# Down projection: running sums copied into accumulator banks by ScalarE, in place of sums on VectorE and by transfers

## Chip, core and metric

The kernel runs on one core of a Trainium2 chip. The metric is device time in microseconds (us) of one execution; lower is better. TensorE (PE) does the matrix products, VectorE (DVE) and ScalarE (ACT) work on tiles, GpSimd (POOL) and SyncE (SP) issue transfers here. Every engine runs its own instructions strictly in the order in which they stand in the program, and an instruction waits until what it reads is written and what it overwrites has been read.

## What is computed

One layer of a diffusion step, for two groups of 128 tokens each (prompt and sample) and a model width of 2048. Cut to what matters:

```python
h  = rms_norm(x, norm1_w) * (1 + sc1) + sh1
qa, ka, va, qb, kb, vb, ga, gb = project_heads(h, w_in, ...)
oa, ob = ...                     # windowed attention, neighbourhood attention
x  = x + g1 * (sigmoid(ga) * (oa @ w_br_a) + sigmoid(gb) * (ob @ w_br_b)) @ w_out
h2 = rms_norm(x, norm2_w) * (1 + sc2) + sh2
x  = x + g2 * (square(relu(h2 @ w_up)) @ w_down)      # w_up 2048x8192, w_down 8192x2048
```

The change lies in the last line. Every fp32 product is made of three matmuls over rounded parts: high x high, high x low, low x high. A weight tile `raw` of 128x1024 is therefore split: ScalarE copies it to `wH` (rounded, L93), VectorE subtracts to get `wL` (L241).

## The kernel before

**Steps.** The whole layer is one list of 456 weight steps, `wsteps`. A step is one 512 KB weight tile: SyncE loads it, ScalarE and VectorE split it, TensorE does 12 matmuls of 128x512 with it. `run()` writes the instructions out step by step. Three tables set the order: `RUN[i]` (how many steps ahead the loads stand), `LOOK[i]` (how many steps ahead the two splitting instructions stand) and `LO_DMA` (steps whose low part is made by a negated copy on ScalarE, L247, and an accumulating transfer issued by GpSimd). `at(i, fn)` places other work behind the matmuls of step i; `load_at(i, fn)` places loads ahead of it. Further tables (`T_PAIR`, `P_PAIR`, `DOTS`, `JOBS` and so on) say at which step smaller pieces of work stand.

**The MLP.** The up projection makes 16 column blocks of 512 (`up0` to `up15`), the down projection consumes them in 8 pieces of two blocks. After block 0 and 1 the program runs in turn: pair p+1 of the up projection (16 steps, some of them in a form with seven products where eight are usual, at the positions in `FAST`), then piece p of the down projection. In the seven-product form, VectorE first makes sums of weight tiles (`t`, `raw`, L1172 to L1182), and TensorE collects in banks `Q1` to `Q7`; at a pair's end the banks are put together into `up` (ScalarE `up<-Q`, then VectorE L1217 and ScalarE's Relu and Square, L1223). The result is turned to stationary form through ScalarE copies (`pla`, `fTa`, `aNH`) and transposing transfers, with VectorE's low parts (`aNL`, L97).

**The down projection.** A piece has four column units n of 512 columns. A unit is 4 steps, 48 matmuls, into two accumulator banks (`acc`, one for each token group). Four banks of the pool `pacc` are handed round among the units and the pairs' first Q banks. The sum over the 8 pieces is kept in SBUF tiles `dsum[n]`. When unit (p, n) is done, `evac` takes its two banks:

- piece 0: ScalarE copies both to `dsum[n]` (L93);
- pieces 1 to 6, the 10 units in `SUM_DMA` (unit number 4p+n): ScalarE copies both to a further tile, and a transfer issued by GpSimd adds that tile to `dsum[n]` (L1261);
- the other 14 units: VectorE adds each bank to `dsum[n]` (L1257);
- behind piece 6, `gate_sum(n)`: VectorE multiplies `dsum[n]` by the gate (L1238) and adds it to the residual `x1[n]` (L1239);
- piece 7: `resid` multiplies the bank by the gate and adds it to `x1[n]` (L904, L905), and the result is stored. The last unit is `last_unit`, which ends with one bank ahead of the other.

The gate tiles (`gate_bc`) and `x1` (`x1_back`) are loaded six steps before the end of each unit of piece 6.

Of the kernel before, what the change touches and what calls it, by code (L numbers as in the profile page):

```python
# [51 lines left out]
XS_AT = {1: 13, 2: 18, 3: 29}  # L52
POST = {('kvA', 0): [67, 70, 75], ('qA', 0): [70, 73, 78], ('qA', 1): [72, 74, 80], ('kB', 0): [77, 83, 90], ('qB', 0): [82, 84, 93], ('kB', 1): [86, 91, 93], ('qB', 1): [90, 93, 97]}
JOBS = [[79, 80, 80, 87, 93], [81, 83, 88, 90, 93], [87, 87, 89, 90, 99], [93, 93, 96, 99, 102], [96, 97, 100, 105, 112], [102, 103, 107, 112, 123], [105, 107, 111, 118, 123], [112, 115, 118, 121, 123]]
SS_AT = [43, 51, 73, 75, 139, 139]
T_AT = [4, 4]
PREP_IN = [6, 7]
DOTS = [33, 39, 42, 43, 47, 47, 48, 49, 52, 54, 55, 57, 60, 62, 69, 70, 73, 77, 80, 84, 90, 91, 92, 92, 94, 98, 101, 103, 103, 105, 108, 110, 111, 112, 115, 118, 120, 121, 122, 122, 126, 127, 128, 129, 130, 132, 132, 136, 137, 138, 138, 143, 144, 147, 147, 150, 153, 155, 157, 161, 164, 167, 170, 172, 173, 174, 175, 176, 177, 178, 179, 182]
DOTS2 = [230, 232, 234, 235, 236, 237, 240, 243, 255, 263, 265, 269, 270, 288, 301, 301, 307, 328, 328, 331, 333, 334, 358, 360, 361, 363, 366, 368, 391, 391, 395, 399]
STAT_AT = [-1, 0, 10, 16]  # L60
T_PAIR = [[8, 9], [6, 8], [8, 9], [7, 8], [10, 11], [8, 9], [12, 11]]
P_PAIR = [[4, 2], [2, 4], [3, 4], [1, 3], [6, 6], [3, 3], [6, 5]]
M_TE = (3,)
# [8 lines left out]
def tile_hybrid_step(ctx: ExitStack, tc: tile.TileContext, a):  # L72
# [210 lines left out]
    def mm3(acc, stat, st, first, last, order=(0, 1)):  # L283

        wh, wl = st["hl"]
        for k in range(2):
            kk = 2 * st["half"] + k
            for tb in order:
                sh, sl = stat(kk, tb)
                f, l = first and k == 0, last and k == 1  # L290
                pe.matmul(acc[tb], sh, wh[:, k, :], start=f, stop=False)  # L291
                pe.matmul(acc[tb], sh, wl[:, k, :], start=False, stop=False)  # L292
                pe.matmul(acc[tb], sl, wh[:, k, :], start=False, stop=l)  # L293
# [219 lines left out]
    def unit(w, c0, ktiles, stat, evac, key, order="both"):  # L513
# [377 lines left out]
    x1 = {}  # L891
# [159 lines left out]
    def last_unit(w, c0, ktiles, stat, evac_s, key):  # L1051
# [4 lines left out]
        def mms(q, tb):  # L1056
            wh, wl = box["hl"][q]
            for k in range(2):
                sh, sl = stat(q // 2)(2 * (q % 2) + k, tb)
                pe.matmul(box["acc"][tb], sh, wh[:, k, :], start=q == 0 and k == 0, stop=False)  # L1060
                pe.matmul(box["acc"][tb], sh, wl[:, k, :], start=False, stop=False)
                pe.matmul(box["acc"][tb], sl, wh[:, k, :], start=False, stop=q == n - 1 and k == 1)

        for j, k0 in enumerate(ktiles):
            def mm(st, j=j):
                q = 2 * j + st["half"]
                if q == 0:
                    box["acc"] = [bank("acc", pacc) for _ in range(2)]
# [38 lines left out]
    def up_pair(p):  # L1107
# [32 lines left out]
        for pos, is_fast in enumerate(kinds):  # L1140
# [50 lines left out]
            def mm_y(st, b=b, j=j, pos=pos, end=end):  # L1191
# [42 lines left out]
    def gate_sum(n):  # L1234

        d = dsum.pop(n)
        for s in range(2):
            dve.tensor_tensor(d[:, s, :], d[:, s, :], gbc["g2", n][:, s, :], op=OP.mult)  # L1238
# [259 lines left out]
```

## Time and profile before

| what | value |
| --- | --- |
| median of 3 runs | 1333.61 us (1331.23, 1333.61, 1334.71) |
| span of the profiled execution | 1331.3 us |
| TensorE busy | 1316.0 us, 99% |
| TensorE weight loads busy (beside matmuls) | 1067.0 us, 80% |
| VectorE busy | 1190.2 us, 89% |
| ScalarE busy | 800.8 us, 60% |
| GpSimd busy | 54.6 us, 4% |
| traffic | 392 MB, mean 295 GB/s |

The span of the profiled execution is its own time from the first to the last instruction, and for this execution it is the only time recorded; it lies 2.3 us under the median of the runs. Matmuls overlap in the records (each shows 0.39 us, the next starts 0.227 us later), so a busy TensorE has to be read by the distance from one start to the next.

### The profile page before, as it was taken

What the parts mean: (1) busy time and instruction counts of PE and PEld (TensorE: products, weight loads), DVE (VectorE), ACT (ScalarE), POOL (GpSimd) and SP (SyncE); (2) the same over time, 40 slices, a digit from 0 to 9 for tenths busy, and PEclk for the clock granted to TensorE, in tenths of its full rate; (3) what the DMA queues carried; (4) which work ended last, traced back from release to release, by engine and by line L of the source; (5) the groups of instructions that cost most, each with busy time, mean ns of one, the idle gap of its engine ahead of it and who ended that gap; (6) DMA issues with size and microseconds to landing.
All of it is one profiled execution on the core that took longest, in us unless ns stands there. A gap on an engine that the chain in (4) does not pass through costs nothing.

```text
span 1331.3 us, 18039 instructions
## 1 busy us (share of the span) xinstructions
PE 1316.0 (99%) x6411; PEld 1067.0 (80%) x6412; DVE 1190.2 (89%) x1546; ACT 800.8 (60%) x979; POOL 54.6 (4%) x64
## 2 busy tenths in 40 slices
PE   8999999999999999999999999999999999999998
PEld 4777778788888878888888888888888888877887
DVE  4699999988898999999779998998999999989685
ACT  5534443476656446635677866758577576676660
POOL 0000000521000000000000000000000000000000
PEclk9999999999999999999999999999999999999999
DMA  9999998986589999996578876988798696878962
GB/s 374 409 409 408 409 401 300 384 277 240 177 329 355 381 392 356 354 367 214 191 230 280 281 254 215 291 273 266 235 296 255 237 301 206 311 195 291 331 213 98
DMA packets 148267, 392.24 MB, mean 295 GB/s; under 512 B 51793, under 2 KB 53009, under 8 KB 148177
## 3 DMA queue, kind: packets, MB, share of 16 engines
q1 hardware_dynamic: 144448, 378.16, 78.8%
q0 software_dynamic: 3584, 12.85, 5.0%
q8 instruction: 50, 0.82, 0.3%
q14 instruction: 41, 0.33, 0.1%
q10 hardware_dynamic: 144, 0.08, 0.0%
HBM read 367.16 MB, written 8.68 MB: 282 GB/s over the span
## 4 chain that ended last, share of the span: by engine, by line
PE 92%; DMA 4%; DVE 2%; ACT 1%; issue 1%; SPq 0%; DVEq 0%; ACTq 0%
PE acc L291 16%; PE acc L292 16%; PE acc L293 16%; PE Q L1117 6%; PE Q L1119 6%; PE Q L1118 6%; PE acc L391 4%; PE acc L392 4%; PE acc L393 4%; DMA araw<-in_w_pair 3%; PE ps_ada L308 2%; PE ps_S L707 1%; PE Z L1119 1%; PE Z L1117 1%; PE Z L1118 1%; DMA aT<-in_w_adaT 1%
## 5 line engine op out<-in xcount | busy, mean ns | idle before, releaser
L241 DVE TENSOR_TENSOR wL<-raw,wH 128x1024 fp32r<-128x1024 f32 x375 | 446.6, 1225 | 72.0 <-ACT wH L93 67.9
L93 ACT ACTIVATE wH<-raw 128x1024 fp32r<-128x1024 f32 (+1 forms) x393 | 392.8, 1044 | 128.3 <-PE acc L392 23.3
L391 PE MATMUL acc<-wH,hH 128*128 128x512 f32 x276 | 109.1, 395 | 0.0
L393 PE MATMUL acc<-wH,hL 128*128 128x512 f32 x276 | 107.5, 390 | 0.0
L392 PE MATMUL acc<-wL,hH 128*128 128x512 f32 x276 | 107.5, 389 | 0.0
L291 PE MATMUL acc<-wH,hH 128*128 128x512 f32 x256 | 101.4, 396 | 0.0
L293 PE MATMUL acc<-wH,hL 128*128 128x512 f32 x256 | 99.7, 390 | 0.0
L292 PE MATMUL acc<-wL,hH 128*128 128x512 f32 x256 | 99.7, 390 | 0.0
L1327 DVE CUSTOM_DVE_ANT_0 aT<-aT,cB,cols 128x1024 f32<-128x1024 f32 x56 | 71.7, 1286 | 0.2
L1327 DVE CUSTOM_DVE_ANT_0 junk<-aT,cB,cols 128x1024 bf16<-128x1024 f32 x56 | 71.4, 1280 | 0.0
L93 ACT ACTIVATE tH<-t 128x1024 fp32r<-128x1024 f32 x33 | 35.0, 1061 | 58.0 <-DVE t L1172 55.4
L391 PEld LDWEIGHTS acc<-wH,hH 128*128 128x128 f32 x276 | 51.8, 188 | 13.6 <-issue 2.5
L393 PEld LDWEIGHTS acc<-wH,hL 128*128 128x128 f32 x276 | 51.8, 188 | 11.0
L392 PEld LDWEIGHTS acc<-wL,hH 128*128 128x128 f32 x276 | 51.8, 188 | 10.4
L293 PEld LDWEIGHTS acc<-wH,hL 128*128 128x128 f32 x256 | 48.0, 188 | 10.2
L291 PEld LDWEIGHTS acc<-wH,hH 128*128 128x128 f32 x256 | 48.1, 188 | 9.8 <-ACT sq L622 0.4
L292 PEld LDWEIGHTS acc<-wL,hH 128*128 128x128 f32 x256 | 48.1, 188 | 9.4
L93 ACT ACTIVATE uH<-raw 128x1024 fp32r<-128x1024 f32 x33 | 35.1, 1063 | 31.6 <-DVE raw L1177 28.6
L1223 ACT ACTIVATE up<-up 128x1024 f32<-128x1024 f32 x28 | 29.7, 1062 | 26.8 <-DVE up L1217 26.3
L308 PE MATMUL ps_ada<-araw,cpad 128*32 128x256 f32 x640 | 39.1, 382 | 2.7 <-DMA araw<-in_w_pair 2.5
L93 ACT ACTIVATE fTa<-pTa 128x2048 uint16<-128x2048 uint16 x16 | 40.5, 2533 | 2.0 <-PE acc L292 1.4
L1172 DVE TENSOR_TENSOR t<-raw 128x1024 f32<-128x1024 f32 x33 | 40.2, 1219 | 1.0 <-PE acc L292 1.0
(641 smaller groups left out, 3316.7 us busy)
## 6 DMA issues: line engine op xcount, KB each, us to landing
raw<-in_w_in SPq DMA_DIRECT2D x133, 512.0 KB, 9.5
raw<-in_w_down SPq DMA_DIRECT2D x128, 512.0 KB, 5.6
araw<-in_w_pair SPq DMA_DIRECT2D x80, 512.0 KB, 10.2
raw<-in_w_upF SPq DMA_DIRECT2D x66, 512.0 KB, 5.2
aT<-in_w_gT SPq DMA_DIRECT2D x64, 512.0 KB, 6.9
raw<-in_w_up SPq DMA_DIRECT2D x62, 512.0 KB, 5.0
aT<-in_w_adaT SPq DMA_DIRECT2D x48, 512.0 KB, 9.6
raw<-in_w_out SPq DMA_DIRECT2D x32, 512.0 KB, 9.6
```

Source lines behind the costliest of these rows:

```text
L93: act.activation(out, in_, AF.Copy)
L241: dve.tensor_tensor(st["lo"], st["raw"], st["hi"].bitcast(F32), op=OP.subtract)
L291: pe.matmul(acc[tb], sh, wh[:, k, :], start=f, stop=False)
L292: pe.matmul(acc[tb], sh, wl[:, k, :], start=False, stop=False)
L293: pe.matmul(acc[tb], sl, wh[:, k, :], start=False, stop=l)
L391: pe.matmul(acc[tb], sh, wh[:, k, :], start=kt == 0 and k == 0, stop=False)
L392: pe.matmul(acc[tb], sh, wl[:, k, :], start=False, stop=False)
L393: pe.matmul(acc[tb], sl, wh[:, k, :], start=False, stop=last and k == 1)
L1117: pe.matmul(acc, stat[0], hi, start=f, stop=False)
L1118: pe.matmul(acc, stat[0], lo, start=False, stop=False)
L1119: pe.matmul(acc, stat[1], hi, start=False, stop=l)
L1327: dve.tensor_tensor_reduce(out, box["raw"], cB[s, tag], 1.0, dst if second else baT[:, part, fb:fb + 1], OP.mult, OP.add, dst)
```

## The change

Unit (p, n) of pieces 1 to 7 no longer starts from empty banks. `seed(p, n)` has ScalarE copy `dsum[n]` into the unit's two banks ahead of its first matmul, and the matmuls go on from there (no `start` flag). So every unit of pieces 0 to 6 ends with the same two ScalarE copies, bank to `dsum[n]`, and the banks of piece 7 hold the sum over all pieces. The adds on VectorE, the accumulating transfers with their tiles, and `gate_sum` go. A seed stands three steps before its unit (`SEED_AT`); that of a piece's first unit stands at the end of the pair before it, between `up<-Q` and Relu, except for piece 7, where it too stands three steps ahead. The gate and residual loads move from piece 6 to nine steps before the end of each unit of piece 7. The tables are new: of the 456 entries each, 25 of `LOOK` and 48 of `RUN` differ, by one to three; the number of seven-product positions in each pair stays; two steps in `LO_DMA` change.

```diff
-FAST = {1: (0, 3, 7), 2: (0, 2, 6, 7), 3: (0, 2, 4, 5, 7), 4: (0, 2, 4, 5, 7), 5: (0, 3, 4, 5, 7), 6: (0, 2, 4, 5, 7), 7: (0, 1, 2, 4, 5, 7)}
-SUM_DMA = [5, 6, 11, 13, 16, 19, 21, 23, 25, 27]
+FAST = {1: (0, 3, 7), 2: (0, 2, 6, 7), 3: (0, 3, 4, 5, 7), 4: (0, 2, 4, 5, 7), 5: (0, 1, 3, 5, 7), 6: (0, 2, 4, 5, 7), 7: (0, 1, 2, 3, 5, 7)}
+SEED_AT = 3
+BACK = 9
-LO_DMA = [70, 83, 107, 131, 176, 184, 233, 292, 314, 328, 402, 404]
+LO_DMA = [70, 83, 107, 119, 131, 176, 184, 233, 292, 314, 393, 404]
-T_PAIR = [[8, 9], [6, 8], [8, 9], [7, 8], [10, 11], [8, 9], [12, 11]]
+T_PAIR = [[8, 9], [6, 8], [6, 9], [7, 8], [10, 13], [8, 9], [12, 14]]
...
     def unit(w, c0, ktiles, stat, evac, key, seeded=None):
...
-                    box["acc"] = [bank("acc", pacc) for _ in range(2)]
-                mm3(box["acc"], stat(j), st, j == 0 and st["half"] == 0, j == n - 1 and st["half"] == 1)
+                    box["acc"] = seeded() if seeded else [bank("acc", pacc) for _ in range(2)]
+                mm3(box["acc"], stat(j), st, j == 0 and st["half"] == 0 and not seeded, j == n - 1 and st["half"] == 1,
+                    bool(seeded))
...
     def up_pair(p):
...
                 if end:
                     for n, u in ((n0, u0), (n1, u1)):
                         up_r[n] = u
+                    if p > 1:
+                        seed(p - 1, 0)
+                    for n, u in ((n0, u0), (n1, u1)):
                         for f in (AF.Relu, AF.Square):
                             act.activation(u.rearrange("p s n -> p (s n)"), u.rearrange("p s n -> p (s n)"), f)
...
-    def gate_sum(n):
-        d = dsum.pop(n)
-        for s in range(2):
-            dve.tensor_tensor(d[:, s, :], d[:, s, :], gbc["g2", n][:, s, :], op=OP.mult)
-            dve.tensor_tensor(x1[n][:, s, :], x1[n][:, s, :], d[:, s, :], op=OP.add)
...
+    def seed(p, n):
+        seeds[p, n] = [bank("acc", pacc) for _ in range(2)]
+        for s in range(2):
+            copy(seeds[p, n][s], dsum[n][:, s, :])
...
     def down_unit(p, n):
         def evac(acc):
-            by_pool = 4 * p + n in SUM_DMA
-            if p == 0 or by_pool:
-                part = G(f"dsum{n}").rearrange("p (s n) -> p s n", s=2)
+            if p == 0:
+                dsum[n] = G(f"dsum{n}").rearrange("p (s n) -> p s n", s=2)
             for s in range(2):
                 if p == last:
                     out_s(acc, n, s)
-                elif p == 0 or by_pool:
-                    copy(part[:, s, :], acc[s])
                 else:
-                    dve.tensor_tensor(dsum[n][:, s, :], dsum[n][:, s, :], acc[s], op=OP.add)
-            if p == 0:
-                dsum[n] = part
-            elif by_pool:
-                pool.dma_start(dsum[n], part, accum_op=OP.add)
+                    copy(dsum[n][:, s, :], acc[s])
+        if p and (n or p == last):
+            at(len(wsteps) - SEED_AT, lambda: seed(p, n))
...
-        e = end_of(("down", last - 1, n))
-        load_at(e - 6, lambda n=n: gate_bc("g2", n))
-        load_at(e - 6, lambda n=n: x1_back(n))
+        e = end_of(("down", last, n))
+        load_at(e - BACK, lambda n=n: gate_bc("g2", n))
+        load_at(e - BACK, lambda n=n: x1_back(n))
```

Three places show how the order of the instructions moves. A number behind a name tells one buffer from another, `x2` is a row that stands twice, and the line numbers of the changed kernel are one to six higher.

First, ScalarE where the fifth pair of the up projection ends and piece 4 of the down projection begins. Before:

```order
L93 ACTIVATE wH<-raw 128x1024 x4
L93 ACTIVATE up_9590<-Q_9277 128x512
L1223 ACTIVATE up_9590<-up_9590 128x1024 x2
L1223 ACTIVATE up_9591<-up_9591 128x1024 x2
L93 ACTIVATE wH<-raw 128x1024 x3
```

After:

```order
L94 ACTIVATE wH<-raw 128x1024 x4
L94 ACTIVATE up_9606<-Q_9304 128x512
L94 ACTIVATE acc<-dsum_6878 128x512 x2
L1228 ACTIVATE up_9606<-up_9606 128x1024 x2
L1228 ACTIVATE up_9607<-up_9607 128x1024 x2
L94 ACTIVATE wH<-raw 128x1024
L94 ACTIVATE acc<-dsum_6971 128x512 x2
```

The first unit's seed, two copies, stands between `up<-Q` and Relu; the second unit's seed stands two rows after the last Square, with one `wH` between.

Second, VectorE at the end of piece 5, where it passes to the weight sums of pair 7. Before:

```order
L97 TENSOR_TENSOR a13L<-fTa_10566,a13H 128x1024
L241 TENSOR_TENSOR wL<-raw,wH 128x1024 x2
L1257 TENSOR_TENSOR dsum_7084<-dsum_7084,acc 128x512 x2
L1172 TENSOR_TENSOR t_10614<-raw 128x1024
L1175 TENSOR_TENSOR raw<-t_10614,raw 128x512
```

After:

```order
L98 TENSOR_TENSOR a13L<-fTa_10588,a13H 128x1024
L242 TENSOR_TENSOR wL<-raw,wH 128x1024 x2
L1174 TENSOR_TENSOR t_10642<-raw 128x1024
L1177 TENSOR_TENSOR raw<-t_10642,raw 128x512
```

The two adds of unit 22 (`dsum_7084`) are gone from between the low parts and the first weight sum `t`.

Third, ScalarE over the same stretch, with the tail of piece 5. Before (`dsum_10517` and `dsum_10694` are the further tiles of units 21 and 23):

```order
L93 ACTIVATE wH<-raw 128x1024 x2
L93 ACTIVATE dsum_10517<-acc 128x512 x2
L93 ACTIVATE fTa_10540<-pTa_10460 128x2x1024
L93 ACTIVATE a12H<-fTa_10540 128x1024
L93 ACTIVATE grow<-ps_gr 32x128
L93 ACTIVATE fTa_10566<-pTa_10462 128x2x1024
L93 ACTIVATE a13H<-fTa_10566 128x1024
L93 ACTIVATE wH<-raw 128x1024 x2
L93 ACTIVATE XH<-raw 128x1024
L93 ACTIVATE YB<-raw 128x512
L93 ACTIVATE tH<-t_10614 128x1024
```

After:

```order
L94 ACTIVATE dsum_6971<-acc 128x512 x2
L94 ACTIVATE fTa_10564<-pTa_10480 128x2x1024
L94 ACTIVATE a12H<-fTa_10564 128x1024
L94 ACTIVATE grow<-ps_gr 32x128
L94 ACTIVATE fTa_10588<-pTa_10482 128x2x1024
L94 ACTIVATE a13H<-fTa_10588 128x1024
L94 ACTIVATE acc<-dsum_7157 128x512 x2
L94 ACTIVATE wH<-raw 128x1024 x2
L94 ACTIVATE XH<-raw 128x1024
L94 ACTIVATE dsum_7085<-acc 128x512 x2
L94 ACTIVATE YB<-raw 128x512
L94 ACTIVATE tH<-t_10642 128x1024
```

Unit 23's seed (`acc<-dsum_7157`) has come in behind `a13H`, and unit 22's evacuation (`dsum_7085<-acc`) between `XH` and `YB`.

More of the change, by code (lines that the diff above doesn't have):

```diff
@@ L65 @@
 FLIP = 1
-P_UP = [4, 1]
+P_UP = [3, 1]
 T_UP = [6, 5]
@@ L281, in run, with mm3 @@
                 fn()
-    def mm3(acc, stat, st, first, last, order=(0, 1)):
+    def mm3(acc, stat, st, first, last, seeded=False):
         wh, wl = st["hl"]
@@ L287, in mm3 @@
             kk = 2 * st["half"] + k
-            for tb in order:
+            for tb in range(2):
                 sh, sl = stat(kk, tb)
                 f, l = first and k == 0, last and k == 1
-                pe.matmul(acc[tb], sh, wh[:, k, :], start=f, stop=False)
-                pe.matmul(acc[tb], sh, wl[:, k, :], start=False, stop=False)
-                pe.matmul(acc[tb], sl, wh[:, k, :], start=False, stop=l)
+                pe.matmul(acc[tb], sh, wh[:, k, :], start=f, stop=False, skip_group_check=seeded)
+                pe.matmul(acc[tb], sh, wl[:, k, :], start=False, stop=False, skip_group_check=seeded)
+                pe.matmul(acc[tb], sl, wh[:, k, :], start=False, stop=l, skip_group_check=seeded)
     def pair_load(box, nsub, fb):
@@ L510, in tile_hybrid_step, with unit @@
     begin()
-    def unit(w, c0, ktiles, stat, evac, key, order="both"):
+    def unit(w, c0, ktiles, stat, evac, key, seeded=None):
         box = {}
@@ L1067, in mm @@
                 if q == 0:
-                    box["acc"] = [bank("acc", pacc) for _ in range(2)]
+                    box["acc"] = seeded()
                 box["hl"][q] = st["hl"]
```

45 lines of the change are left out of this document (25 added, 20 removed).

## Prediction

> **What bounds the kernel now.** I read the page's busy times first, then a table of stretches (busy time of each engine, granted TensorE clock, share of the transfer engines), then TensorE's waits behind the up projection's first block, then the timeline where such a wait is long.
>
> ```profile
> PE 1316.0 (99%) x6411; PEld 1067.0 (80%) x6412; DVE 1190.2 (89%) x1546; ACT 800.8 (60%) x979; POOL 54.6 (4%) x64
> 45.00:774.00 729.00, 728.75 (x3738) 594.08 (x3737) 673.10 (x942) 418.59 (x571) 39.58 (x39) 1.00 0.88 322
> 774.00:1195.00 421.00, 420.49 (x1853) 346.96 (x1852) 394.07 (x452) 289.44 (x297) 10.40 (x12) 1.00 0.79 256
> 1195.00:1204.00 9.00, 5.40 (x18) 4.02 (x17) 8.86 (x11) 5.61 (x7) 0.87 (x1) 0.81 0.91 282
> 1204.00:1326.00 122.00, 122.00 (x539) 100.75 (x538) 94.44 (x105) 64.44 (x66) 1.72 (x2) 1.00 0.74 238
> PE Q L1117 <- ACT dsum L93: 4.0, 2, 3.6
> ```
>
> TensorE is the bound: 420.49 of 421 us before 1195, all of 122 us behind 1204. What the change can win is only what TensorE loses from the first seeded unit on. The wait list has one row there, 4.0 us in two waits, on ScalarE's evacuations (L93). They lie here:
>
> ```profile
> 943.48 0.39 PE L1119 MATMUL Q<-YB,h20L 128*128 128x512 f32 x1
> 944.26 0.50 PE L1117 MATMUL Q<-tH,sH 128*128 128x512 f32 x1 [0.40 <-ACT dsum L93]
> 859.43 0.39 PE L1119 MATMUL Q<-YB,h20L 128*128 128x512 f32 x1
> 859.93 0.50 PE L1117 MATMUL Q<-tH,sH 128*128 128x512 f32 x1
> 1195.58 0.39 PE L1119 MATMUL Q<-YB,h20L 128*128 128x512 f32 x1
> 1199.57 0.80 PE L1117 MATMUL Q<-tH,sH 128*128 128x512 f32 x1 [3.60 <-ACT dsum L93]
> 1200.16 0.63 PE L1118 MATMUL Q<-tL,sH 128*128 128x512 f32 x1
> ...
> 1202.99 0.40 PE L1119 MATMUL Q<-tH,sL 128*128 128x512 f32 x1
> ```
>
> Matmuls start 0.227 us apart when nothing is late (rows 1066.97 to 1067.65 below: 0.68 for three). So the losses are 3.99 - 0.23 = 3.76 us at 1195.8; 0.55 at 943.7; 0.27 at 859.7. Behind the longest idle the clock is halved: the eight starts from 1199.57 to 1202.99 take 3.42 us where eight cost 1.81, a further 1.61. Sum: 6.2 us. That is the ceiling; nothing the change touches holds TensorE elsewhere.
>
> By the Trainium skill ("TensorE: Matmul & The Clock Gate", Part 1: The HAM clock gate), the clock halves after an idle window of some 3.4 us and needs as long a busy one to return; the trace agrees, with 3.60 us idle and some 3.4 us slow, and no slow row behind the 0.40 us idle at 944.26.
>
> **Part by part.** *Counts and engine time.* Groups of the whole trace (busy us, mean ns):
>
> ```profile
> L1257 DVE TENSOR_TENSOR dsum<-dsum,acc 128x512 f32<-128x512 f32 x28 | 18.2, 683 | 2.7 <-PE acc L293 2.7
> L1239 DVE TENSOR_TENSOR x1b<-x1b,dsum 128x512 f32<-128x512 f32 x8 | 5.5, 692 | 0.3
> L1238 DVE TENSOR_TENSOR dsum<-dsum,g 128x512 f32<-128x512 f32 x8 | 5.5, 685 | 0.0
> L93 ACT ACTIVATE dsum<-acc 128x512 f32<-128x512 f32 x28 | 16.0, 594 | 24.3 <-PE acc L293 22.5 <-PE acc L292 1.2
> L93 ACT ACTIVATE YB<-raw 128x512 fp32r<-128x512 f32 x33 | 20.5, 620 | 2.8 <-DMA raw<-in_w_upF 2.6
> dsum<-dsum POOLq DMA_DIRECT2D x10, 512.0 KB, 6.9
> ```
>
> VectorE loses 28 adds and 16 gate operations: 29.2 us. ScalarE gains 28 x 2 seed copies and 48 - 20 evacuating copies: 84, at 0.53 us each (a pair of `dsum` copies takes 1.06 at 1198.94 below), 45 us. It is 69% busy from 774 to 1195 (289.44 of 421), so this goes to about 78%; neither moves the end by itself, since TensorE is at 100%. Ten transfers go; no wait of TensorE in this part names a transfer, so they give nothing (they would give if the 0.79 share held a weight load, which no row shows).
>
> No copy from SBUF to a PSUM bank stands in the trace. The bounds are 0.53 (bank to SBUF, in a pair) and 0.62 (`YB`, SBUF to SBUF). I take 0.53, since a pair runs back to back. The Trainium skill ("ScalarE: Activation LUTs", Step-by-step: what each stage is for) calls ScalarE's way into PSUM the faster port, useful only if TensorE doesn't need most of PSUM. It gives no figure; the rows' 0.53 would then be high, and the caveat speaks against this change.
>
> *The stall at 1196.* Its chain, ScalarE then VectorE:
>
> ```profile
> 1175.10 1.09 ACT L93 ACTIVATE dsum<-acc 128x512 f32<-128x512 f32 x2 [1.16 <-PE acc L292]
> 1183.27 2.00 ACT L93 ACTIVATE wH<-raw 128x1024 fp32r<-128x1024 f32 x2
> 1195.92 1.06 ACT L93 ACTIVATE tH<-t 128x1024 fp32r<-128x1024 f32 x1 [2.02 <-DVE t L1172]
> 1197.97 1.06 ACT L93 ACTIVATE uH<-raw 128x1024 fp32r<-128x1024 f32 x1 [1.00 <-DVE raw L1177]
> 1198.94 1.06 ACT L93 ACTIVATE dsum<-acc 128x512 f32<-128x512 f32 x2
> 1184.54 2.35 DVE L241 TENSOR_TENSOR wL<-raw,wH 128x1024 fp32r<-128x1024 f32 x2
> 1186.81 1.28 DVE L1257 TENSOR_TENSOR dsum<-dsum,acc 128x512 f32<-128x512 f32 x2
> 1188.01 1.22 DVE L1172 TENSOR_TENSOR t<-raw 128x1024 f32<-128x1024 f32 x1
> 1194.60 1.22 DVE L1172 TENSOR_TENSOR t<-raw 128x1024 f32<-128x1024 f32 x1
> ```
>
> Unit 23's banks are due at 1195.81 for Q7, but their evacuation (1198.94) stands behind `uH`, which waits for VectorE, whose second `t` at 1194.60 follows a full row of sums behind the first at 1188.01. The adds of unit 22 took 1.20 us of that row (1186.81 to 1188.01) and go. Ahead of it ScalarE gets unit 23's seed (+0.97, a pitch), and loses the 1.16 it stood at 1175.10, where it waited for a matmul in the middle of unit 22, so not for its own bank but for the further tile, which seeding doesn't need; so `wH` at 1183.27 comes 0.2 us sooner at best, and I count 0.1. Unit 22's evacuation (1.06) moves in front of `YB`, which VectorE reads only 1.9 us behind `t`: hidden; it costs up to 0.5 if that slack is gone. So VectorE and unit 23's evacuation come 1.3 us sooner: stall 2.4 us, saving 1.3.
>
> An idle of about 2.2 us then stands where 3.60 halved the clock. Its nearest rows are 0.40 (clock kept) and 3.60 (halved); I take it as kept, saving 1.6, and keep 0 as the other end. By the Trainium skill (the clock gate's page and section, as above) the window is 3413 ns and free-running, so 2.2 us can't fill one: it gives the same 1.6.
>
> *The two small stalls.* The weight loads of the same matmuls name VectorE's adds too:
>
> ```profile
> L1117 PEld LDWEIGHTS Q<-tH,sH 128*128 128x128 f32 x60 | 11.5, 192 | 7.9 <-ACT dsum L93 4.8 <-DVE dsum L1257 0.5 <-ACT wH L93 0.3
> ```
>
> That is 859.7, where a bank waits for the adds of unit 7; at 943.7 it is unit 11's evacuation, in row behind `XH`. Both become copies in ScalarE's row; the second keeps its place behind `XH`. I take half of 0.27 + 0.55 back: 0.4 (bounds 0 and 0.8).
>
> *Seeds at a pair's end.* A bank of a pair must be read before it can be seeded: the first by `up<-Q`, the second by VectorE's first sum.
>
> ```profile
> 1065.81 0.60 ACT L93 ACTIVATE up<-Q 128x512 f32<-128x512 f32 x1 [0.30 <-PE Q L1119]
> 1066.78 2.72 DVE L1217 TENSOR_TENSOR up<-up,Q 128x512 f32<-128x512 f32 x4
> 1066.97 0.39 PE L291 MATMUL acc<-wH,a8H 128*128 128x512 f32 x1
> ...
> 1067.65 0.40 PE L291 MATMUL acc<-wH,a8H 128*128 128x512 f32 x1
> 813.46 2.80 DVE L1217 TENSOR_TENSOR up<-up,Q 128x512 f32<-128x512 f32 x4
> 815.46 0.39 PE L291 MATMUL acc<-wH,a2H 128*128 128x512 f32 x1
> ```
>
> The first sum ends at 1066.78 + 0.68 = 1067.46, the seed behind it some 0.6 later at 1068.06, and the unit's second bank is due at 1067.65: 0.4 us new. Nobody else is held much: behind the seed stand Relu and Square, which wait for the last of the four sums at 1069.5. The second pair stands for the other four seeded ends: 813.46 + 0.70 + 0.6 = 814.8, due at 815.46, in time by 0.7.
>
> *Other seeds* stand three steps, 36 matmuls or 8.2 us, ahead, behind ScalarE's other work. The tightest:
>
> ```profile
> 820.88 3.89 ACT L93 ACTIVATE wH<-raw 128x1024 fp32r<-128x1024 f32 x4
> 825.66 0.39 PE L291 MATMUL acc<-wH,a2H 128*128 128x512 f32 x1
> 928.00 2.94 ACT L93 ACTIVATE wH<-raw 128x1024 fp32r<-128x1024 f32 x3
> 931.46 0.39 PE L291 MATMUL acc<-wH,a4H 128*128 128x512 f32 x1
> ```
>
> Piece 1's second unit: seed at 824.7, first bank ready at 825.3, due at 825.66. Piece 2's last: its ScalarE row gains two seeds and an evacuation by then (2.9 us), against idle time of about as much in front: no slack left. I put 0.4 on all (0 to 2). Late seeds also hold what queues behind them, `wH` and the transposed copies, but those stand two or more steps ahead of use.
>
> *Loads.* Gate and residual tiles come nine steps, 24 us, ahead of a unit's end, where landing takes under 10 us: hidden. If not, only the last unit's tail would pay. The first seconds of loading, whose order stays, and the tail stay as they are.
>
> Sum: 1.3 + 1.6 + 0.4 - 0.4 - 0.4 = 2.5 us. Against the profiled execution that is 1331.3 - 2.5 = 1328.8; its span is 2.3 us under the median of the runs, so on that scale 1333.6 - 2.5 = **1331.1**.
>
> **The rivals.** A measurement of this kernel can tell about 0.3%, 4 us, from no change.
>
> *All stalls go.* VectorE, 29 us lighter, reaches pair 7's first sums so early that unit 23 is evacuated in time: 6.2 - 0.2 for the seed at 1067 gives 1327.6. For it: VectorE's work goes exactly where the chain stands. Against: the second `t` follows the first by 6.6 us of sums that stay, and those start behind ScalarE's `wH`. Chance 0.20.
>
> *The stall stays.* ScalarE's seed and evacuation in front of pair 7 eat the 1.2 us, or the half clock comes with 2.4 us of idle; with 0.8 for seeds: 1333.5. For it: ScalarE sits on both ends of that chain. Chance 0.17.
>
> *The other side: ScalarE late with seeds.* A seed is on TensorE's path, an evacuation by VectorE was not. In an in-order ScalarE at 78%, which stands still where `tH` and `uH` wait for VectorE (2.02 and 1.00 above), seeds come late. From 0.3 us of delay (the slack at 825.66) each piece pays; 0.5 at the pair's end and 1.0 at one later unit for six pieces is 9 us, less the 0.8 counted: 1339.3. For it: slack near nothing at two units. Against: the two units are the tightest I found, and the new tables could move `wH` out of the way. Chance 0.16. The Trainium skill's caveat on PSUM, above, points to this side.
>
> **The numbers.** The forecast has 0.47, its own range 1329.0 to 1333.0. The range 1327.0 to 1337.5 leaves out about the outer half of the last rival and a little below the first. Faster than 1329.6: 0.18 of the first rival and 0.12 of the forecast, 0.30. Slower than 1337.6: 0.14 of the last. Same: 0.56.
>
> **What would show it.** In the profile after: the wait of a `Q` matmul on ScalarE's `dsum` near 1196 at about 2.2 us with the clock at 1.00 (right), gone (first rival), over 3.4 with half clock (second). Waits of `acc` matmuls on ScalarE's `acc<-dsum`: about 1 us in all, one at pair 5's end (right), or several of a microsecond (last rival). VectorE at about 1161 us, ScalarE at 846. I am wrong if the seed copy takes clearly more than 0.6 us, or if a load becomes what TensorE waits for.

## The result: slower by 0.23%, and the profile after

The changed kernel takes 1335.74 us (median of 11 runs, 1334.75 to 1339.35), the kernel before 1333.53 us (median of 11, 1331.23 to 1334.71): ratio 1.0023, 95% interval 1.0015 to 1.0031. The forecast was 2.5 us faster; the kernel is 2.2 us slower, inside the range but on the other side of no change. The profiled execution has a span of 1335.1 us against 1331.3, 3.8 us more. The device time of a profiled execution lies some 1.8 us above its span (here 1336.9, 1.2 above the median), so spans compare with spans.

The page's busy times and the table of stretches, at the bounds used before (the last stretch is 4 us longer, to the same point of the program):

```profile
PE 1316.1 (99%) x6412; PEld 1065.7 (80%) x6412; DVE 1163.9 (87%) x1502; ACT 843.1 (63%) x1063; POOL 46.7 (4%) x54
45.00:774.00 729.00, 725.35 (x3722) 591.02 (x3721) 666.99 (x937) 415.88 (x567) 41.27 (x40) 1.00 0.88 322
774.00:1195.00 421.00, 419.40 (x1845) 345.10 (x1844) 381.21 (x427) 321.04 (x362) 3.45 (x4) 1.00 0.75 248
1195.00:1204.00 9.00, 6.95 (x31) 5.43 (x29) 8.90 (x11) 5.14 (x7) 0.00 (x0) 1.00 0.49 175
1204.00:1330.00 126.00, 125.28 (x551) 103.41 (x552) 86.47 (x90) 78.18 (x90) 0.00 (x0) 1.00 0.65 225
```

VectorE and ScalarE came out as counted (1161 and 846 forecast). TensorE is idle for 3.6 us between 45 and 774 us, where it had lost 0.25, in front of the first seeded unit. What it waits for over the whole span (us in total, times, longest); the rows left out, for loads and sums in the first part, stood before too with the same sizes within 0.1 us:

```profile
PE ps_gr L1346 <- DVE gc_g L1333: 3.6, 2, 2.9
PE Q L1119 <- ACT dsum L94: 2.5, 2, 2.1
PE ps_sel L327 <- ACT S L94: 1.0, 2, 0.5
PE acc L293 <- DVE wL L242: 0.7, 1, 0.7
PE acc L292 <- ACT acc L94: 0.4, 1, 0.4
```

The largest is new and lies at 494 us, in the attention output's projection. TensorE's timeline, then ScalarE's and VectorE's ahead of it:

```profile
494.62 0.39 PE L294 MATMUL acc<-wH,oLA 128*128 128x512 f32 x1
497.93 0.27 PE L1346 MATMUL ps_gr<-ident,gc_g 128*32 128x128 f32 x1 [2.92 <-DVE gc_g L1333]
486.63 1.06 ACT L94 ACTIVATE wH<-raw 128x1024 fp32r<-128x1024 f32 x1 [3.44 <-DMA raw<-in_w_br_a]
489.19 1.06 ACT L94 ACTIVATE wH<-raw 128x1024 fp32r<-128x1024 f32 x1 [1.50 <-DMA raw<-in_w_br_a]
487.73 1.23 DVE L242 TENSOR_TENSOR wL<-raw,wH 128x1024 fp32r<-128x1024 f32 x1 [3.06 <-ACT wH L94]
490.29 1.23 DVE L242 TENSOR_TENSOR wL<-raw,wH 128x1024 fp32r<-128x1024 f32 x1 [1.33 <-ACT wH L94]
```

`ps_gr` transposes the gate's column sums `gc_g`, made by VectorE in `dots`. VectorE stood waiting for two `wH`, and these for branch weights still in flight; before, ScalarE waited for such a weight once in that stretch, for 1.28 us. By delay (the distance from the start before, less 0.227 us) that is 3.1 us. With 0.7 us at 269 (`ps_sel`), 0.4 at 343 and 0.3 in the first 45 us, less small gains, the first seven-product matmul starts 4.0 us later. That row and the last matmul, before and then after:

```profile
688.98 0.39 PE L1117 MATMUL Q<-XH,h20H 128*128 128x512 f32 x1
1326.32 0.39 PE L1062 MATMUL acc<-wH,a15L 128*128 128x512 f32 x1
692.93 0.39 PE L1119 MATMUL Q<-XH,h20H 128*128 128x512 f32 x1
1330.09 0.39 PE L1064 MATMUL acc<-wH,a15L 128*128 128x512 f32 x1
```

From the first to the second it is 637.2 us, against 637.3 before: **in this profile all of the 3.8 us is lost in front; the down projection, with all that was changed in it, gains 0.2 us where 2.5 were forecast.**

Inside it, the gains came nearly as forecast, and losses that the sum did not have took them back. The stall at 1196 (6 us later on this clock) is down to 2.10 us idle, 2.26 of delay, and the clock stayed full; pair 5's end shows two small delays, 0.13 and 0.25 us, one at the first matmul into each of the seeded banks (TensorE's timeline):

```profile
1201.56 0.39 PE L1121 MATMUL Q<-YB,h20L 128*128 128x512 f32 x1
1204.05 0.50 PE L1119 MATMUL Q<-tH,sH 128*128 128x512 f32 x1 [2.10 <-ACT dsum L94]
1204.38 0.40 PE L1120 MATMUL Q<-tL,sH 128*128 128x512 f32 x1
...
1071.41 0.39 PE L1121 MATMUL Q<-XH,sL 128*128 128x512 f32 x1
1071.76 0.50 PE L292 MATMUL acc<-wH,a8H 128*128 128x512 f32 x1
...
1072.33 0.39 PE L294 MATMUL acc<-wH,a8L 128*128 128x512 f32 x1
1072.81 0.50 PE L292 MATMUL acc<-wH,a8H 128*128 128x512 f32 x1
```

New, and not in the sum: 0.8 us at the second `ps_gr` (0.1 before), and 0.8 at the last piece's first unit (0.1 before); and a late seed in piece 1 that is bigger than assumed (0.57 at 851). TensorE's timeline at the first two, then ScalarE's and TensorE's in piece 1:

```profile
1182.91 0.39 PE L294 MATMUL acc<-wH,a10L 128*128 128x512 f32 x1
1183.97 0.28 PE L1346 MATMUL ps_gr<-ident,gc_g 128*32 128x128 f32 x1 [0.67 <-DVE gc_g L1333]
1288.50 0.40 PE L292 MATMUL acc<-wH,a14H 128*128 128x512 f32 x1
1289.57 0.50 PE L293 MATMUL acc<-wL,a14H 128*128 128x512 f32 x1 [0.67 <-DVE wL L242]
843.58 1.06 ACT L94 ACTIVATE wH<-raw 128x1024 fp32r<-128x1024 f32 x1 [0.90 <-DMA raw<-in_w_down]
...
851.32 1.10 ACT L94 ACTIVATE acc<-dsum 128x512 f32<-128x512 f32 x2
851.95 0.50 PE L292 MATMUL acc<-wH,a2H 128*128 128x512 f32 x1 [0.41 <-ACT acc L94]
```

### The profile page after: what moved, and what is told of

It is laid out like the page before. It is cut to its first block, busy times and chain, and to the rows that moved or that the text cites. A ratio compares the mean times of both kernels' runs of the same rounds, so it can differ in the third digit from the quotient of the medians.

```text
span 1335.1 us, 18036 instructions
## 1 busy us (share of the span) xinstructions
PE 1316.1 (99%) x6412; PEld 1065.7 (80%) x6412; DVE 1163.9 (87%) x1502; ACT 843.1 (63%) x1063; POOL 46.7 (4%) x54
## 4 chain that ended last, share of the span: by engine, by line
PE 82%; DMA 9%; ACT 5%; DVE 2%; issue 2%; SPq 0%; POOL 0%; ACTq 0%; DVEq 0%; POOLq 0%
PE acc L292 13%; PE acc L293 13%; PE acc L294 13%; PE Q L1119 6%; PE Q L1121 6%; PE Q L1120 6%; PE acc L392 4%; PE acc L393 4%; PE acc L394 4%; DMA araw<-in_w_pair 4%; ACT wH L94 2%; PE ps_ada L309 1%; ACT fTa L94 1%; PE ps_S L709 1%; PE Z L1119 1%
## 5 line engine op out<-in xcount | busy, mean ns | idle before, releaser
L94 ACT ACTIVATE acc<-dsum 128x512 f32<-128x512 f32 x56 | 31.7, 590 | 14.8 <-DVE t L906 8.6
L1333 DVE CUSTOM_DVE_ANT_0 aT<-aT,cB,gc_g 128x1024 f32<-128x1024 f32 x32 | 40.7, 1282 | 0.2
```

The lines of the kernel that those rows point to most:

```text
L94: act.activation(out, in_, AF.Copy)
L1333: dve.tensor_tensor_reduce(out, box["raw"], cB[s, tag], 1.0, dst if second else baT[:, part, fb:fb + 1], OP.mult, OP.add, dst)
```

## The experiments

Each time is a median; the ratio is to the kernel before on the same chip. "Old" is an entry of the kernel before, "new" one of the changed kernel; "front" is all that acts ahead of weight step 208. Beside the table entries that the diff of the change shows, the changed kernel has new entries in `GATE_BACK`, `XS_AT`, `POST`, `JOBS`, `SS_AT`, `DOTS`, `M_AT` and `P_UP` (all front), and in `DOTS2` and `P_PAIR` (behind it).

**Where the loss is made: front tables, both ways round.**

a_front_old: the changed kernel with the old front.

```diff
-GATE_BACK = 6
+GATE_BACK = 8
-SS_AT = [48, 51, 75, 75, 139, 139]
+SS_AT = [43, 51, 73, 75, 139, 139]
...
```

> The changed kernel, but every table entry that acts ahead of weight step 208 (first MLP block and all in front of it) as in the kernel before: GATE_BACK, XS_AT, POST, JOBS, SS_AT, DOTS, M_AT, P_UP, LO_DMA and the first 208 entries of LOOK and RUN. Theory 1 (the loss is made in front of the down projection, by loads that the new tables place later): the wait of ps_gr on VectorE's gc_g near 494 us, 2.9 us, goes; 1335.7 - 3.7 = 1332.0 us, 1.5 below the kernel before. Theory 2 (the loss is ScalarE's in the down projection, the wait at 494 is an accident of one execution): 1335.7 us, no change against the changed kernel.

1337.06 us, ratio 1.0031 (1.0019 to 1.0042): not faster. But the wait at 494 is gone, and the first seven-product matmul is back at 688.70 us. What was won there was lost again behind 1280 us, in piece 7's first unit. ScalarE's row, then TensorE's:

```profile
1275.79 2.54 ACT L94 ACTIVATE fTa<-pTa 128x2048 uint16<-128x2048 uint16 x1 [2.64 <-DMA pTa<-pla]
1285.94 0.50 PE L292 MATMUL acc<-wH,a14H 128*128 128x512 f32 x1 [1.73 <-ACT wH L94]
1287.20 0.50 PE L293 MATMUL acc<-wL,a14H 128*128 128x512 f32 x1 [0.76 <-DVE wL L242]
```

ScalarE stands 2.64 us for block 14's transposing transfer; the next weights' `wH` and `wL` queue behind it. TensorE loses 2.9 us, and runs at half clock for 3.4 us after. In the changed kernel that transfer cost ScalarE 0.57 us. So neither theory was right as it stood: the front loss is there, and there is a second one.

b_front_new: the kernel before with the new front, and nothing else.

```diff
-GATE_BACK = 8
+GATE_BACK = 6
-SS_AT = [43, 51, 73, 75, 139, 139]
+SS_AT = [48, 51, 75, 75, 139, 139]
...
```

> The kernel before, with the changed kernel's table entries for all ahead of weight step 208 and nothing else of the change. Theory 1: 1333.5 + 3.7 = 1337.2 us, with a wait of ps_gr on gc_g of about 2.9 us near 494. Theory 2: 1333.5 us and no such wait.

1337.0 us, ratio 1.0026 (1.0014 to 1.0038): 3.6 us slower, the wait at 494 is 1.8 us, and the first seven-product matmul starts at 691.51, 2.5 us later than before. Behind it, the half clock near 1201 lasts 6.8 us in this profile, where it was 3.4 before. Theory 1 holds in the old kernel: the front tables alone make it slower by more than the whole change does.

a_all_old: the seeds in the old tables throughout.

```diff
-T_PAIR = [[8, 9], [6, 8], [6, 9], [7, 8], [10, 13], [8, 9], [12, 14]]
+T_PAIR = [[8, 9], [6, 8], [8, 9], [7, 8], [10, 11], [8, 9], [12, 11]]
...
```

> The seeds alone: the changed kernel's code with every table of the kernel before. Theory 1: no loss in front; near 1196 a wait of 2.4 us without half clock, seeds 1 to 2 us in all: 1331.5 to 1333.0 us. Theory 2: without the tables that make room for the seeds ScalarE is later still: 1337 us or more, with acc matmuls waiting for ScalarE's acc copies for 3 us or more in all.

1339.33 us, ratio 1.0048 (1.0035 to 1.0060), the slowest. Front as before (688.97); `acc` matmuls wait for ScalarE's seeds 3.9 us in four waits, and the stall at 1196 is 2.8 us with half clock. This is the last rival of the prediction in kind. That the time falls on its 1339.3 is in part luck: the seeds' delays add up to 5 us in this profile, not to 9, and the rest is gain of the forecast that did not come (the half clock, most of the stall). With the new tables in the down projection 0.4 us of these waits is left in the changed kernel's profile, 2.7 in the next one's.

a_gate8: the changed kernel with one entry old.

```diff
-GATE_BACK = 6
+GATE_BACK = 8
```

> The changed kernel with GATE_BACK 8 as before (gate tiles fetched back from memory eight steps ahead of use, not six), all else as changed. If the third gate tile's load, which now stands behind the eight loads for the modulation at 457 to 467 us, in front of branch weights, is what makes VectorE late at 494: the wait of 2.9 us goes to under 1, and 1333 us. If it is the branch and gate weights loaded one step later (RUN at 111 to 122, 134, 135): unchanged, 1335.7 us.

1337.06 us, ratio 1.0033 (1.0020 to 1.0045): no gain, though the wait at 494 shrank from 2.9 to 0.4 us and the first seven-product matmul starts at 690.14. Its profile, of the longest of its five executions (1338.84 us), shows what else can happen in the same code, on ScalarE and TensorE in piece 1 (timeline):

```profile
843.23 1.06 ACT L94 ACTIVATE wH<-raw 128x1024 fp32r<-128x1024 f32 x1 [3.36 <-DMA raw<-in_w_down]
...
848.35 0.39 PE L294 MATMUL acc<-wH,a3L 128*128 128x512 f32 x1
851.47 0.50 PE L292 MATMUL acc<-wH,a2H 128*128 128x512 f32 x1 [2.72 <-ACT acc L94]
```

One weight load takes 6.7 us from issue to landing, 4.2 in the changed kernel's profile. These 2.5 us make ScalarE late, and the seed behind it makes TensorE late by 2.9 us, with 3.4 us at half clock behind. Before, ScalarE's waits for the same loads (1.06 and 0.70 us) reached nobody.

**The tail and the lead of the seeds.** f_seed4: a_front_old with `SEED_AT` 4.

```diff
-SEED_AT = 3
+SEED_AT = 4
```

> The kernel with the changed code and the old tables in front (a_front_old), and seeds four steps ahead of their unit instead of three. Theory S (a seed puts ScalarE's row, with its waits for weight loads, on TensorE's path, so 2.7 us more lead takes the late seeds away): the waits near 847 and 931 (0.46 and 0.13 us of delay there) go, those at pair 5's end (1067) stay; 0.6 us less than a_front_old in the sums of the profile, 1335 to 1337 us. Rival: a seed this early waits for its banks, holds up ScalarE's row and with it wH; a new wait of acc on wH or wL, 1338 us or more.

1338.54 us, ratio 1.0048 (1.0034 to 1.0061). The late seeds of pieces 1 and 2 are gone from its profile, as theory S says, and a new delay of 0.46 us on a `wL` came at 1085.26; the tail's stall is there as in a_front_old. No gain by time while that stands.

f_tail: a_front_old with pair 7's two old entries.

```diff
-T_PAIR = [[8, 9], [6, 8], [6, 9], [7, 8], [10, 13], [8, 9], [12, 14]]
+T_PAIR = [[8, 9], [6, 8], [6, 9], [7, 8], [10, 13], [8, 9], [12, 11]]
-P_PAIR = [[4, 2], [2, 4], [3, 4], [3, 3], [6, 6], [3, 3], [9, 5]]
+P_PAIR = [[4, 2], [2, 4], [3, 4], [3, 3], [6, 6], [3, 3], [6, 5]]
```

> a_front_old with the old table entries for pair 7's result (T_PAIR and P_PAIR: copies and transposes of block 14 and 15 two to three steps sooner). Theory T (the wait for block 14's transposed tile near 1284, 1.9 + 1.0 us of delay and 1.8 of half clock behind it in the profile of a_front_old, comes from these two entries): that wait falls under 0.3 us, nothing else moves: 1337.1 - 3.5 = 1333.6 us. Rival (it comes from the gate and residual loads, which now stand among piece 7's loads in SyncE's row): the wait stays, 1337 us.

1333.69 us, ratio 1.0006 (0.9997 to 1.0015): 3.4 us less than a_front_old, where 3.5 was expected, and the tail's stall is 0.3. The gate and residual loads, which stayed where the change put them, do not make it. With seeds four steps ahead the same entries make 5.6 us (f_seed4 1338.54, the next kernel 1332.96, both on one chip). In a_front_old's profile block 14's transfer takes 10.9 us from issue to landing, in f_tail's 4.3.

f_tail_seed4: both.

```diff
-SEED_AT = 3
+SEED_AT = 4
...
-T_PAIR = [[8, 9], [6, 8], [6, 9], [7, 8], [10, 13], [8, 9], [12, 14]]
+T_PAIR = [[8, 9], [6, 8], [6, 9], [7, 8], [10, 13], [8, 9], [12, 11]]
...
```

> Both edits, seeds four steps ahead and the old entries for pair 7. If both theories hold: 1332.5 us, with 2.0 us idle near 1197 and 0.7 at ps_gr as the largest waits left behind 774 us. If either fails: 1335 us or more.

1332.96 us, ratio 1.0001 (0.9992 to 1.0010): the same as the kernel before. So with the old front and pair 7's old entries the seeds, with the other new tables behind the front, come out even, and the forecast's 2.5 us is missing here too. Its profile gains 1.6 us at the stall and 1.6 of half clock; 0.9 more at `ps_gr`, 0.4 at pair 5's end, 0.6 at two `wL`, 0.2 at 945 and the restarts behind them take most of it back.

a_tail: the changed kernel with pair 7's two old entries, front new.

```diff
-T_PAIR = [[8, 9], [6, 8], [6, 9], [7, 8], [10, 13], [8, 9], [12, 14]]
+T_PAIR = [[8, 9], [6, 8], [6, 9], [7, 8], [10, 13], [8, 9], [12, 11]]
...
```

> The changed kernel with the old T_PAIR and P_PAIR entries for pair 7 and nothing else. The wait of a14's wL near 1288 (0.84 us of delay in the profile) falls under 0.3. Theory T2 (the tail costs the changed kernel as much as a_front_old in most executions, and its profiled one was a lucky one): 1335.7 - 3 = 1332.7 us. Rival (it costs what that profile shows): 1335.7 - 0.7 = 1335.0 us.

1337.25 us, ratio 1.0035 (1.0023 to 1.0047): no gain either. Its profile (span 1333.4) is of an execution 2 us under the median and shows the tail mended and the front lost (2.2 us at 494). The granted clock on record is 1.000 for the two executions near 1335 us and 0.996 for the one at 1340.9; 0.004 of 1335 us is some 5 us, so most of that spread is time at half clock. Where it falls, no trace here shows.

**Which part of the front.** Four kernels split it in the kernel before, two in the seeded one.

b_gate6: the kernel before, gate tiles back two steps later.

```diff
-GATE_BACK = 8
+GATE_BACK = 6
```

> The kernel before with GATE_BACK 6 instead of 8 and nothing else: the third gate tile's load moves from in front of the eight modulation loads to behind them, among the branch weights. Theory G (that load is most of the front loss): ps_gr waits on gc_g near 494 for 1.5 to 2.5 us, 1332.7 + 2 = 1334.7 us. Rival (the loss needs the lower RUN entries): no such wait, 1332.7 us.

1333.13 us, ratio 0.9999 (0.9990 to 1.0008); no wait at 494. Theory G falls.

b_run: the kernel before with the new front entries of `RUN` (when the weight loads stand).

```diff
-RUN = "3011100000000102122233333222...
+RUN = "0000000000000001133233333222...
```

> The kernel before with the changed kernel's first 208 entries of RUN (26 loads' lead times: those of the first steps, and one step less at 111 to 122, 134, 135 and 170 to 177) and nothing else. Theory R (branch weights loaded later make VectorE late at 494): ps_gr waits there on gc_g for 1 to 2 us, 1333.4 + 1.5 = 1335 us. Rival (the loss is in the places of the gate and modulation sums): 1333.4 us, no such wait.

1332.81 us, ratio 1.0000 (0.9991 to 1.0008); no wait at 494. b_run_gate: both.

```diff
-RUN = "3011100000000102122233333222...
+RUN = "0000000000000001133233333222...
-GATE_BACK = 8
+GATE_BACK = 6
```

> RUN as in b_run, and GATE_BACK 6. Theory RG (the two together: the gate tile's load takes the place among branch weights that are late already): the whole wait of b_front_new at 494, 1.8 us or more, 1333.4 + 2.5 = 1336 us. Rival: no more than b_run.

1332.73 us, ratio 1.0001 (0.9992 to 1.0010); no wait at 494. Later loads alone cost nothing. b_rest: all other front entries new.

```diff
-LO_DMA = [70, 83, 107, 131, 176, 184, 233, 292, 314, 328, 402, 404]
+LO_DMA = [70, 83, 107, 119, 131, 176, 184, 233, 292, 314, 328, 402, 404]
-XS_AT = {1: 13, 2: 18, 3: 29}
+XS_AT = {1: 13, 2: 16, 3: 30}
...
```

> The kernel before with all of the changed kernel's front tables but RUN and GATE_BACK (XS_AT, POST, JOBS, SS_AT, DOTS, M_AT, P_UP, LO_DMA 119, LOOK). If loads alone make the wait at 494: none here, but the small losses near 269 and 343 us (0.6 and 0.4), 1334.4 us. If the places of the sums make it: 1.5 us or more at 494, 1336 us.

1334.48 us, ratio 1.0014 (1.0005 to 1.0022): 1.5 us slower, with 0.4 us at 494. The same split in the seeded kernel, f_tail_seed4 with the new front, whole (n_tail_seed4) and its loads alone (n_loads_only):

```diff
-GATE_BACK = 8
+GATE_BACK = 6
-SS_AT = [43, 51, 73, 75, 139, 139]
+SS_AT = [48, 51, 75, 75, 139, 139]
...
```

> The changed kernel with the old entries for pair 7 and seeds four steps ahead: f_tail_seed4 with the new tables in front. Theory F (the front tables cost 3 to 4 us whatever stands behind): the first Q matmul starts near 692.5 us, not 689.2; 1333.0 + 3.5 = 1336.5 us. Rival (the front's delay is made up later): 1333.5 us.

```diff
-GATE_BACK = 8
+GATE_BACK = 6
-RUN = "3011100000000102122233333222...
+RUN = "0000000000000001133233333222...
```

> f_tail_seed4 with the new RUN and GATE_BACK in front, all other front tables old. Theory P (the loss in front comes from the places of the small work, DOTS, JOBS, POST, SS_AT and the like, not from the loads' lead): first Q matmul at 689 to 690 us, 1333.0 to 1334.0 us. Rival (the loads' lead costs in the seeded kernel): 692 us, 1336 us.

n_tail_seed4 1337.05 us, ratio 1.0034 (1.0022 to 1.0046); n_loads_only 1332.85, ratio 1.0004 (0.9996 to 1.0013). The first seven-product matmul of each, n_tail_seed4 first:

```profile
691.46 0.39 PE L1119 MATMUL Q<-XH,h20H 128*128 128x512 f32 x1
```

```profile
689.17 0.39 PE L1119 MATMUL Q<-XH,h20H 128*128 128x512 f32 x1
```

Shown: the new places of the small work in front (`DOTS`, `JOBS`, `POST`, `SS_AT`, `XS_AT`, `M_AT`, `P_UP`, the new step in `LO_DMA` and nine `LOOK` entries) make the loss. They cost 1.5 us with the old loads (b_rest) and 4.2 with the new ones (n_tail_seed4 against n_loads_only, one chip). The loads' lead alone costs nothing, but with the places the wait at 494 grows from 0.4 to 1.6 us and more. Of the 4.2 us, 2.3 stand in front of the first seven-product matmul; most of the rest is a half clock of 3.4 us near 1203 that n_loads_only's profile does not have. Which single place does it was not tried.

**The stall at 1196, without seeds.** b_unit22: the kernel before with one more unit in the list.

```diff
-SUM_DMA = [5, 6, 11, 13, 16, 19, 21, 23, 25, 27]
+SUM_DMA = [5, 6, 11, 13, 16, 19, 21, 22, 23, 25, 27]
```

> The kernel before with unit 22 added to SUM_DMA: its two adds on VectorE, which stand in front of pair 7's first weight sum, become two copies on ScalarE and a transfer. Nothing is seeded. Theory (the stall at 1195.8 ends when VectorE's row ends, the half clock behind it goes with it): idle 3.6 falls to 2.4, clock 1.00, 1333.4 - 2.8 = 1330.6 us. Rival (the stall hangs on something else, or ScalarE's two copies take the time back): idle 3 or more with half clock, 1333.4 us.

1330.98 us, ratio 0.9985 (0.9976 to 0.9993), 1.7 us faster where 2.8 were expected. The idle time fell to 2.3 us as worked out; the half clock came all the same. TensorE's timeline, then the table of stretches (the clock is the last column but two):

```profile
1197.25 0.50 PE L1117 MATMUL Q<-tH,sH 128*128 128x512 f32 x1 [2.32 <-ACT dsum L93]
...
1199.13 0.63 PE L1118 MATMUL Q<-tL,sH 128*128 128x512 f32 x1
```

```profile
1194.00:1206.00 12.00, 9.68 (x36) 7.50 (x35) 11.90 (x14) 8.73 (x11) 0.86 (x1) 0.86 0.93 267
```

b_look: the kernel before with one number changed, so that unit 23's evacuation stands in front of the second block's `YB`, `tH` and `uH`.

```diff
@@ LOOK, entry 406
-5
+4
```

> The kernel before with one entry of LOOK smaller by one (step 406: 5 to 4): the splitting of pair 7's second seven-product block (YB, tH, uH) now stands behind unit 23's evacuation on ScalarE, not in front of it; nothing else moves. Theory E (the stall at 1195.8 is only a matter of order in ScalarE's row: the bank is full at 1194.5 and its copy stands behind waits for VectorE): the wait of 3.6 us and the half clock go; a small new wait for the second block's parts, up to 1.5 us, since VectorE's 6.6 us for each such block are longer than TensorE's 5.4: 1332.7 - 4 = 1328.7 us. Rival (VectorE is the bound of this stretch): the wait only moves to the second block's tL and uL, 3 us or more there: 1332 us or more.

1331.16 us, ratio 0.9985 (0.9976 to 0.9994): 2.3 us faster. ScalarE empties the bank 5.2 us sooner, and TensorE runs through; then it waits for VectorE's `XL` (ScalarE's timeline, then TensorE's):

```profile
1193.71 1.28 ACT L93 ACTIVATE dsum<-acc 128x512 f32<-128x512 f32 x2 [0.59 <-PE acc L293]
1195.33 0.39 PE L1119 MATMUL Q<-YB,h20L 128*128 128x512 f32 x1
1195.56 0.39 PE L1117 MATMUL Q<-tH,sH 128*128 128x512 f32 x1
...
1205.40 0.50 PE L1118 MATMUL Q<-XL,h21H 128*128 128x512 f32 x1 [1.30 <-DVE XL L1180]
```

Theory E holds for the stall, and half of the rival with it: part of it moves on to VectorE (1.5 us at `XL`, 0.5 at a `wL`). b_u22_look: both edits.

```diff
@@ LOOK, entry 406
-5
+4
-SUM_DMA = [5, 6, 11, 13, 16, 19, 21, 23, 25, 27]
+SUM_DMA = [5, 6, 11, 13, 16, 19, 21, 22, 23, 25, 27]
```

> Both small edits to the kernel before: unit 22's sum by copies and transfer, and LOOK one smaller at step 406. Theory E: VectorE another 1.2 us earlier, so the new wait at the second block goes too: 1327.5 us. If VectorE is the bound of the stretch: 1330 us, as unit 22's edit alone.

**1329.84 us, ratio 0.9971 (0.9961 to 0.9981): 3.6 us faster than the kernel before, the fastest version here.** That is nearer to the 1330 of the rival than to the 1327.5 of theory E: the wait at `XL` is halved, not gone, and the adds of unit 7 hold TensorE for 0.9 us near 860. TensorE's waits behind 774 us:

```profile
PE Q L1117 <- DVE dsum L1257: 0.9, 1, 0.9
PE Q L1118 <- DVE XL L1180: 0.8, 2, 0.6
PE acc L292 <- DVE wL L241: 0.6, 1, 0.6
```

f_look: f_tail_seed4 with the same entry.

```diff
@@ LOOK, entry 406
-5
+4
```

> The seeded kernel with the old tables in front and for pair 7, seeds four steps ahead (f_tail_seed4), and LOOK one smaller at step 406. Theory E: the 2.0 us of idle near 1198, and the half clock that follows it in some executions, go: 1333.0 - 2.8 = 1330.2 us, 2.5 under the kernel before but not under unit 22's edit with LOOK: seeds give nothing of their own. Rival (seeds pay by the lighter VectorE once this is out of the way): 1328 us or less.

1333.07 us, ratio 1.0000 (0.9991 to 1.0009): the wait near 1198 went, and 2.3 us at `XL` came in two waits behind it. No gain, where 2.8 was expected; the seeded kernel's lighter VectorE does not show in this stretch.

## Why the prediction was wrong, point by point

- **The step that failed is "nothing the change touches holds TensorE elsewhere", with the opening loads' "order stays" taken for the whole front.** The tables are part of the change and act on 690 us in front of the first seed. The sum has no term for them and gives no reason, though the table of stretches showed the transfer engines at 0.88 and VectorE at 673 of 729 us there; and even of the first 19 entries of `RUN`, eight are new. Measured by time: 3.6 us in the kernel before (b_front_new), 4.2 in the seeded one (n_tail_seed4 against n_loads_only). That is more than the whole result; with it the sum would have been 1.1 to 1.7 us slower in place of 2.5 faster. By the first seven-product matmul the front itself is 4.0 us in the changed kernel's profile and 2.5 and 2.3 in these two; the rest of theirs came behind it, as more time at half clock.
- **The sum inside the down projection failed too**: 2.5 us forecast, 0.2 in the profile (637.34 to 637.16). The gains were there, 1.5 at the stall, 1.6 by the clock, 0.25 at the small stalls. Against them stand 0.4 at pair 5's end and 0.7 at other seeds; and, in no term, 0.7 at `ps_gr`, 0.7 at block 14's `wL`, 0.3 at a `wL` near 911 and about 0.4 in restarts.
- **Pair 7's entries**, also at nothing: 3.4 us with the old front (f_tail against a_front_old), 0.8 of delay in the changed kernel's profile. They move block 14's transposing transfer three steps later, from five to two steps (5.4 us) ahead of the copy that reads it, and such a transfer took up to 10.9 us. In the changed kernel itself, mending the front or the tail alone gave no gain, mending both gave some 2 us; why the two losses do not add is open. Time at half clock is a part of it (a_tail), but one profile for each kernel does not show the rest.
- **The stall at 1196**: right. 2.4 us of delay forecast, 2.26 measured; VectorE without unit 22's adds, 1.2 us forecast, and b_unit22 took 1.28 off the idle time (3.60 to 2.32) by that edit alone. b_look shows that the stall also goes by ScalarE's order alone, which the prediction took as given.
- **The half clock**: wrong to count as gone. It kept away in the changed kernel's profile (1.6 us gained) and in six others with as much idle time, and came in two (last section). So its staying away was in part luck.
- **Seeds at a pair's end**: right, 0.4 forecast; 0.13 and 0.25 of delay. The matmul behind each of these, and behind the other small waits, is some 0.1 us late again, which the sum left out.
- **Other seeds**: 0.4 forecast; 0.57 and 0.12 in the profile, 2.9 in a_gate8's, 3.9 waited in the old tables. Under-sized: the slack was reckoned from ScalarE's rows in one execution, and a seed hands ScalarE's wait for a load on to TensorE.
- **The small stalls**: 0.4 forecast to come back, 0.2 did (0.58 left at 948, none at 860). `ps_gr` near 1183, not counted, cost 0.7 more: VectorE waits 0.9 and 0.8 us for `wH` ahead of the sums that it transposes, and on ScalarE a seed's two copies stand between those `wH`.
- **The seed copy's price**: 0.53 forecast; 0.55 in a pair (1.10), and 590 ns mean by the groups of the whole trace, level with the evacuation's and a little under `YB`'s 620:

```profile
L94 ACT ACTIVATE acc<-dsum 128x512 f32<-128x512 f32 x56 | 31.7, 590 | 14.8 <-DVE t L906 8.6 <-DVE up L1219 6.0
L94 ACT ACTIVATE dsum<-acc 128x512 f32<-128x512 f32 x56 | 31.0, 589 | 12.1 <-PE acc L294 11.3
```

- **The rivals**: the last one, seeds late in ScalarE's row, is what the change is without its tables (a_all_old, 6.0 us slower), at some half of the cost that it put on the seeds. In the changed kernel's profile it makes about 1 us. The front as a place of loss stood in none of them.

## What to carry to other kernels

When a change comes with new order tables, cost every stretch on which they act, not only the one that the change is about; in a stretch where VectorE and the transfers are near full, tables that move small work by a few steps can cost more than a good idea brings (4.2 us here, against a forecast of 2.5). A wait on an in-order engine is cheap as long as nobody waits for that engine: before a copy is put on the bounding engine's path, list what stands ahead of it in its row, loads included. And where a bank is full but not emptied, look first at what stands in front of the copy: one number, which let it go ahead of three instructions, two of which wait for VectorE, gave 2.3 us, as much as was forecast for the whole change.

## What the runs showed of the hardware

The half clock does not follow from the length of an idle time alone. Near 1196 us, TensorE's row behind the idle time and the granted clock of the stretch around it (the last column but two), for f_tail (two fences) and then f_tail_seed4 (two), and last TensorE's row in n_tail_seed4, where the clock of the same stretch was 0.87:

```profile
1199.93 0.79 PE L1119 MATMUL Q<-tH,sH 128*128 128x512 f32 x1 [2.04 <-ACT dsum L94]
```

```profile
1194.00:1206.00 12.00, 9.96 (x38) 7.80 (x37) 11.86 (x14) 6.96 (x10) 0.00 (x0) 0.86 0.60 199
```

```profile
1200.77 0.50 PE L1119 MATMUL Q<-tH,sH 128*128 128x512 f32 x1 [1.96 <-ACT dsum L94]
```

```profile
1194.00:1206.00 12.00, 10.04 (x45) 7.95 (x44) 11.86 (x14) 6.96 (x10) 0.00 (x0) 1.00 0.65 206
```

```profile
1202.83 0.77 PE L1119 MATMUL Q<-tH,sH 128*128 128x512 f32 x1 [1.95 <-ACT dsum L94]
```

2.04 and 1.95 us halved the clock, 1.96 did not, and 2.92 us at 494 in the changed kernel did not either (the rows behind it are 0.23 apart). Of the nine profiles with 1.95 to 2.10 us of idle at this place, these two show the half clock and seven do not; 2.32 (b_unit22), 2.78 (a_all_old) and 3.6 us here all brought it. It then lasted 3.4 us, and 6.8 in b_front_new and b_run (granted clock 0.50 throughout). The Trainium skill ("TensorE: Matmul & The Clock Gate", Part 1: The HAM clock gate) gives a free-running window of 3413 ns and one idle window as the condition. That the window runs free fits the scatter; that it must be idle throughout does not fit 1.95 us. So from about 2 us on, an idle time may cost this kernel another 1.6 to 3 us, as it seems by chance: a reason to remove it, and no ground to count the cost as gone.
